# Full 128-row operands in the attention scores and the mLSTM selector, and the PV products of two heads issued together, in a two-layer decoder trunk

## The chip, the core and the metric

The kernel runs on one NeuronCore of a Trainium2 chip. The metric is the device time of one execution in microseconds (us). The kernel before took 924.36 us, the median of three runs (923.03 to 927.12). All durations below come from the profile of one execution of it.

The engines have short names: PE multiplies matrices (PEld is its loading of weights, which overlaps with the multiplying), DVE, ACT and POOL work elementwise, and SP starts the transfers of weights.

## What is computed

Two layers work on 256 tokens of width 1024. Each layer is a mixer (a matrix memory of 4 heads, called mLSTM, beside a sliding-window attention of 16 heads with 4 key heads) and an MLP. The part that matters here:

```python
def mixer_block(h, ...):
    proj = h @ w_in                       # D_MODEL x 6664
    ...
    hm = mlstm_chunkwise(mq, mk, mvf, ig, logf)
    ...
    ha = sliding_window_attention(aq..., ak..., av..., sinks, rel_bias)
    y = sigmoid(ga) * (hm @ w_branch_m) + sigmoid(gb) * (ha @ w_branch_a)
    return y @ w_out

def sliding_window_attention(q, k, v, sinks, rel_bias):   # 16 heads of 64, window 128
    scores = einsum(q, k) * A_HEAD_DIM ** -0.5
    logits = where(valid, scores + bias, -inf)
    m = maximum(max(logits), sink)
    p = exp(logits - m)
    denom = sum(p) + exp(sink - m)
    out = einsum(p / denom, v)
```

## The kernel before

**Products.** Every float32 operand of the large products is held as two float32r parts, high and low, and each product is three matmuls: high by high, low by high, high by low (L211 to L213 with 512 columns moving per matmul, L225 to L227 with 256; together they are called the stream below). ACT makes the high part of a piece of weights (L142), DVE the low part (L117; POOL does one piece of a layer), four pieces ahead of PE.

**Slots.** The program is a list of slots. A slot holds 24 stream matmuls of 256 columns or 12 of 512. Other work is tied to slots by number and is written ahead of the slot's products, so every engine's order is fixed by hand. `s_qk` is the first slot of the memory's queries and keys, and "slot n" below means `s_qk + n`.

**Attention.** Head h goes through four steps, with `heads_at` giving its slot:

- `att1` at slot `heads_at[h]`: four matmuls for the scores (L811 to L814), then bias, sink and maximum on DVE (L819, L821), and the exponentials on ACT (L824 to L826).
- `att2` one slot later: the division, on DVE and POOL (L832 to L835).
- `att3` three slots later: three transposes on PE (L841) and a copy of the result to a tile PT, on ACT (L846), or on DVE for heads 0 and 14 (L844). There are three PT tiles.
- `att4` four slots later: PT times the values, two float32 matmuls for each head (L858, L859), each of which the chip runs as two passes. The result of an even head lies in columns 0 to 63 of the array, that of an odd head in columns 64 to 127. Four heads fill one accumulator, which is then copied and split.

Scores, transposes and PV accumulators share four PSUM tiles, the "B" tiles.

**Operands of the scores.** In the tile q, the 64 rows of a head hold the high part of its queries, and the other 64 rows hold their low part. The tile `kh` holds the same high keys in both halves, so one matmul of 128 rows (L811, L813) gives high by high plus low by high. The low keys `kl` also stand in both halves, but L812 and L814 read only the head's own 64 rows.

**The memory's selector.** `mem1` of each of the 4 memory heads, at slots `s_ga + 2h + 1`, starts with a matmul of `sel` and `Rs` over 64 rows (L877). Rows 0 to 3 and 32 to 35 carry values; the others are zero. The four gates that feed `Rs` are computed on DVE around slots 4 to 6 (`gates2`, L690 to L705) and transposed on PE in slot 6 (`gates3`, L712, L713).

Of the kernel before, what the change touches and what calls it, by code (L numbers as in the profile page):

```python
# [12 lines left out]
F32R = mybir.dt.float32r  # L13
# [4 lines left out]
P = 128  # L18
T = 256
# [23 lines left out]
def trunk(ctx: ExitStack, tc: tile.TileContext, x, norm_mix_g, w_in, conv_w, conv_b, b_igate, b_fgate,  # L43
          mlstm_norm_g, attn_sinks, rel_bias, w_branch_m, w_branch_a, w_out, norm_mlp_g, w_up, w_down,
          final_norm_g, out):
    nc = tc.nc
    const = ctx.enter_context(tc.tile_pool(name="const", bufs=1))
# [19 lines left out]
    def tmp():  # L67
        return act.tile([P, 512], F32, tag="tmp", bufs=4, name=nm("tmp"))
# [12 lines left out]

# [1 line left out]
    N_RAW, N_SPL, AHEAD = 4, 7, 4  # L83
    pieces, pc, last_use, raws = [], {}, {}, {}
# [69 lines left out]

# [1 line left out]
    slots = []  # L156
# [3 lines left out]
    def slot(units, post=()):  # L160
        """units: list of (pieces needed, emit)."""
        slots.append((units, list(post)))
        i = len(slots) - 1
        for need, _ in units:
            for p_ in need:
                last_use[p_] = i
        return i
# [32 lines left out]

# [1 line left out]
    def xs(st, key, xT, pid, kt, tt, hf, first, last, w0=0, n=512):  # L202
        """st[key][:, :n] (+)= x[tt] @ n columns of a piece."""

        def emit():
            xh, xl = st[xT]
            wh, wl = pc[pid]
            b = st[key][:, :n]
            s = slice(tt * P, (tt + 1) * P)
            c = slice(w0 + hf * 512, w0 + hf * 512 + n)  # L210
            nc.tensor.matmul(b, xh[:, kt, s], wh[:, c], start=first, stop=False)  # L211
            nc.tensor.matmul(b, xh[:, kt, s], wl[:, c], start=False, stop=False)  # L212
            nc.tensor.matmul(b, xl[:, kt, s], wh[:, c], start=False, stop=last)  # L213

        return ([pid], emit)

    def ws(st, key, half, xT, pid, kt, wc, first, last):
        """half of st[key] (+)= (x @ 128 columns of a piece)^T, both token tiles."""

        def emit():  # L220
            xh, xl = st[xT]
            wh, wl = pc[pid]
            o = st[key][:, half * T : (half + 1) * T]
            c = slice(wc, wc + P)
            nc.tensor.matmul(o, wh[:, c], xh[:, kt, :], start=first and half == 0, stop=False, skip_group_check=True)  # L225
            nc.tensor.matmul(o, wh[:, c], xl[:, kt, :], start=False, stop=False, skip_group_check=True)  # L226
            nc.tensor.matmul(o, wl[:, c], xh[:, kt, :], start=False, stop=last, skip_group_check=True)  # L227

        return ([pid], emit)
# [4 lines left out]
    def xs_group(st, bkey, xT, w, c0, head="k", tail="k", k0=0, first=True, last=True, alloc=True):  # L234
        """8 slots; returns the first slot's index. head/tail: the order within kts 0-3 / 4-7."""
        pid = [piece(w, k0 + k, c0) for k in range(8)]
        start = len(slots)
# [28 lines left out]
    def ws_group(st, bkey, xT, w, c0, tail="b", head="k"):  # L266
        """8 slots; head/tail: the order within kts 0-3 / 4-7, by kt or by bank."""
        start = len(slots)
# [31 lines left out]

# [1 line left out]
    def evac_split(pt, hi, lo, scale=None):  # L302
# [17 lines left out]
    class Norm:  # L320
        """x * rsqrt(mean(x^2) + eps) * g for one token tile, in steps."""

# [26 lines left out]

# [1 line left out]
    X = const.tile([P, 2, D], F32, name="X")  # L351
# [15 lines left out]
    mask = const.tile([P, P], BF16, name="mask")  # L367
    sel = const.tile([64, 4], F32R, name="sel")
    Rs = const.tile([64, 384], F32R, name="Rs")
    cw = const.tile([P, 80], F32, name="cw")  # L370
# [33 lines left out]
    def setup_small():  # L404
# [4 lines left out]
        z = tmp()  # L409
        nc.gpsimd.memset(z, 0.0)  # L410
        nc.scalar.copy(Rs, z[:64, 0:384])
        for r in (0, 32):
            nc.gpsimd.affine_select(out=z[r : r + 32, 0:4], in_=z[r : r + 32, 0:4], pattern=[[-1, 4]],
                                    compare_op=ALU.not_equal, fill=1.0, base=0, channel_multiplier=1)
        nc.scalar.copy(sel, z[:64, 0:4])
        S0["b8"] = big8()
# [41 lines left out]

# [1 line left out]
    def boundary(st_prev, bkey, prev, st, xkey, nxt, gkey, xtag):  # L460
        """prev: first of the 4 closing slots (tile 0 half 0, 0/1, 1/0, 1/1); nxt: first slot that reads xT."""

# [51 lines left out]
    def first_norm(st, xtag, nxt):  # L514
        """The first norm's gain is applied per channel, after the transposes."""
        xh, xl = st["hT"] = xT_tiles(xtag)
# [63 lines left out]

# [1 line left out]
    def mixer(l, ta, tb):  # L582
        w = w_in[l]
        st = {}
# [11 lines left out]

        # attention keys and values, and both gates
        s_kv = len(slots)
        for k2 in range(4):
            pid = kv_piece(w, k2)  # L600
            units = []
            for kk in range(2):
                kt, w0 = 2 * k2 + kk, kk * 520
                f, e = kt == 0, kt == 7
# [27 lines left out]

        # attention queries
        s_aq = ws_group(st, "aq", "hT", w, AQ0)
# [19 lines left out]

        # gates of the matrix memory: log forget gates, running sums and maxima
        def s24():
# [66 lines left out]

        # memory queries and keys: causal convolution along time, then silu times two
        s_qk = ws_group(st, "qk", "hT", w, 0, tail="k", head="p")
# [33 lines left out]

        # output gate of the matrix memory  # L760
        s_mo = xs_group(st, "mo", "hT", w, MO0, tail="th")
# [42 lines left out]

        # sliding-window attention: a head goes through its four steps in five slots
        def att1(h):
            g, hs = h // 4, slice((h % 2) * 64, (h % 2) * 64 + 64)
            q, kh, kl = st[("q", h // 8)][:, h % 2 * 4 + h % 8 // 2, :], st["kh"], st["kl"]
            gk = g % 2 * 2 + g // 2
            sp = psB()  # L810
            nc.tensor.matmul(sp[:, 0:P], q[:, 0:P], kh[:, gk, 0:P], start=True, stop=False, skip_group_check=True)  # L811
            nc.tensor.matmul(sp[:, 0:P], q[hs, 0:P], kl[hs, gk, 0:P], start=False, stop=True, skip_group_check=True)  # L812
            nc.tensor.matmul(sp[:, P : 3 * P], q[:, P:T], kh[:, gk, :], start=False, stop=False, skip_group_check=True)  # L813
            nc.tensor.matmul(sp[:, P : 3 * P], q[hs, P:T], kl[hs, gk, :], start=False, stop=True,  # L814
                             skip_group_check=True)
            L = act.tile([P, 384], F32, tag="L", bufs=5, name=nm("L"))
# [31 lines left out]

        def att4(h):
            g, hh, hs = h // 4, h % 4, slice((h % 2) * 64, (h % 2) * 64 + 64)  # L850
            if h == 0:
                st["haT"] = xT_tiles(tb)
            if hh == 0:
                st["pv"] = psB()
            pv, PT, va, haT = st["pv"], st[("att", h)], st["va"], st["haT"]
            o = pv[hs, (hh // 2) * T : (hh // 2 + 1) * T]
            vs = slice(g * 64, (g + 1) * 64)
            nc.tensor.matmul(o, va[:, 0, vs], PT[:, 0:T], start=(hh < 2), stop=False, skip_group_check=True)  # L858
            nc.tensor.matmul(o[:, P:T], va[:, 1, vs], PT[:, T:384], start=False, stop=True, skip_group_check=True)  # L859
            if hh == 3:  # L860
                evac_split(pv.rearrange("p (m t) -> p m t", m=2), haT[0][:, 2 * g : 2 * g + 2, :],
                           haT[1][:, 2 * g : 2 * g + 2, :])

        heads_at = (2, 3, 4, 6, 7, 8, 8, 10, 11, 15, 15, 16, 16, 18, 19, 22)
        for h in range(16):
            at_late(s_qk + heads_at[h], lambda h=h: att1(h))
        steps = [(heads_at[h] + j, 4 - j, f, h) for h in range(16) for j, f in ((1, att2), (3, att3), (4, att4))]
        for i, _, f, h in sorted(steps, key=lambda t: (t[0], t[1], t[3])):
            at(s_qk + i, lambda f=f, h=h: f(h))

        # matrix memory, all chunks at once
        sc = 0.25 * 128.0 ** -0.5

        def mem1(h):
            cols, qk = st["cols"], st["qkT"]
            pw = psB()
            nc.tensor.matmul(pw[:, :384], sel[:, h : h + 1].to_broadcast([64, P]), Rs, start=True, stop=False,  # L877
                             skip_group_check=True)
# [5 lines left out]
            sp = psB()  # L884
            nc.tensor.matmul(sp[:, 0:T], qk[:, 4 + h, 0:P], qk[:, h, :], start=True, stop=True,
                             skip_group_check=True)
            nc.tensor.matmul(sp[:, T:384], qk[:, 4 + h, P:T], qk[:, h, P:T], start=False, stop=True,
                             skip_group_check=True)
# [66 lines left out]

# [1 line left out]
    def mlp(l, ta, tb):  # L957
# [68 lines left out]
    prev = None  # L1026
    firsts = []
    for l in range(DEPTH):
# [8 lines left out]
        prev = (stp, s_t)  # L1037
# [5 lines left out]

    # final norm
    stp, s_t = prev
# [50 lines left out]
```

## Time and profile before

| | |
|---|---|
| median of three runs | 924.36 us |
| lowest and highest run | 923.03, 927.12 us |
| span of the profiled execution | 924.4 us (its time is given only as this span) |
| mean granted TensorE clock | 0.994 |
| costliest group on DVE: low parts, L117 | 329.5 us in 274 |
| costliest group on ACT: high parts, L142 | 286.3 us in 280 |

How to read it: a matmul's duration in the trace includes the way through the array, and matmuls overlap. What a matmul costs is the distance from its start to the start of the next. In a row of the timeline the columns are the start, the duration, the engine, the line, the operation, the tiles written and read, the rows and columns of the operands, and the count; the bracket is idle time ahead of the instruction and what ended it.

### The profile page before, as it was taken

Reading aid. Unit: us, or ns where it says so; the run is one execution under the profiler, and the core shown is the slowest. Engines: PE = TensorE matmul, PEld = TensorE weight load, DVE = VectorE, ACT = ScalarE, POOL = GpSimd, SP = SyncE. Lnnn points to the kernel's source line nnn. Section 1 sums busy time; section 2 is a strip of 40 time slices with the busy share of each in tenths; the row PEclk is TensorE's granted clock in tenths of the full one; section 3 lists DMA queues with packets and bytes.
Section 4 is the critical chain, followed back from the end, with each engine's and each line's share of the span. In section 5 each row is a group of like instructions: output and inputs, shape, how many; then the busy total and the mean of one; then the engine's idle time right before and its main releaser. Section 6 shows DMA issues by size and latency. Waiting matters only on the chain.

```text
span 924.4 us, 14901 instructions
## 1 busy us (share of the span) xinstructions
PE 907.8 (98%) x5837; PEld 804.3 (87%) x5837; DVE 574.9 (62%) x922; ACT 469.0 (51%) x769; POOL 137.0 (15%) x179
## 2 busy tenths in 40 slices
PE   8899999999999999999999999999999999999996
PEld 6789878999988999999889987789999889999985
DVE  6647677766677646464665676686666666546462
ACT  6465466655444635354445546666543454545351
POOL 3272343211000000000000533231200000000000
PEclk9999999999999999999999999999999999999999
DMA  7975252444555666464746444243455576565631
GB/s 233 248 231 182 92 154 75 138 138 145 199 176 157 212 206 212 154 227 138 236 134 205 157 149 126 92 144 113 165 154 179 182 228 218 166 212 169 214 115 46
DMA packets 46406, 155.27 MB, mean 168 GB/s; under 512 B 7192, under 2 KB 7296, under 8 KB 46336
## 3 DMA queue, kind: packets, MB, share of 16 engines
q1 hardware_dynamic: 44256, 148.46, 50.2%
q0 software_dynamic: 1792, 5.34, 2.2%
q8 instruction: 46, 0.75, 0.3%
q10 hardware_dynamic: 288, 0.52, 0.1%
q14 instruction: 24, 0.20, 0.1%
HBM read 153.23 MB, written 1.07 MB: 167 GB/s over the span
## 4 chain that ended last, share of the span: by engine, by line
PE 90%; DMA 3%; DVE 3%; issue 2%; POOL 1%; ACT 1%; POOLq 0%; SPq 0%; ACTq 0%; DVEq 0%
PE pa L211 12%; PE pa L212 12%; PE pa L213 12%; PE pa L225 10%; PE pa L226 9%; PE pa L227 9%; PE pb L226 5%; PE pb L225 5%; PE pb L227 5%; PE pb L858 2%; DMA raw<-in_w_in 1%; PE pb L841 1%; DMA b<-ed 1%; PE pb L813 1%; PE pb L313 1%
## 5 line engine op out<-in xcount | busy, mean ns | idle before, releaser
L117 DVE TENSOR_TENSOR lo<-raw,hi 128x1024 fp32r<-128x1024 f32 (+1 forms) x274 | 329.5, 1224 | 144.8 <-ACT hi L142 143.9
L142 ACT CAST hi<-raw 128x1024 fp32r<-128x1024 f32 (+1 forms) x280 | 286.3, 1049 | 179.4 <-PE pa L213 46.2
L225 PE MATMUL pa<-xh,hi 128*128 128x256 f32 x800 | 231.7, 290 | 4.1 <-ACT vm L593 2.8
L227 PE MATMUL pa<-xh,lo 128*128 128x256 f32 x800 | 225.4, 282 | 0.8 <-DVE lo L117 0.8
L226 PE MATMUL pa<-xl,hi 128*128 128x256 f32 x800 | 226.0, 283 | 0.0
L211 PE MATMUL pa<-hi,xh 128*128 128x512 f32 (+1 forms) x416 | 163.5, 393 | 0.1
L212 PE MATMUL pa<-lo,xh 128*128 128x512 f32 (+1 forms) x416 | 160.8, 387 | 0.7 <-DVE lo L117 0.7
L213 PE MATMUL pa<-hi,xl 128*128 128x512 f32 (+1 forms) x416 | 160.4, 386 | 0.0
L225 PEld LDWEIGHTS pa<-xh,hi 128*128 128x128 f32 x800 | 152.1, 190 | 8.1 <-ACT vm L593 3.2
L227 PEld LDWEIGHTS pa<-xh,lo 128*128 128x128 f32 x800 | 152.0, 190 | 1.0 <-DVE lo L117 1.0
L226 PEld LDWEIGHTS pa<-xl,hi 128*128 128x128 f32 x800 | 152.3, 190 | 0.3
L225 PE MATMUL pb<-xh,hi 128*128 128x256 f32 x384 | 108.2, 282 | 0.0
L226 PE MATMUL pb<-xl,hi 128*128 128x256 f32 x384 | 107.5, 280 | 0.0
L227 PE MATMUL pb<-xh,lo 128*128 128x256 f32 x384 | 107.4, 280 | 0.0
L213 PEld LDWEIGHTS pa<-hi,xl 128*128 128x128 f32 x416 | 78.3, 188 | 16.8
L212 PEld LDWEIGHTS pa<-lo,xh 128*128 128x128 f32 x416 | 78.4, 189 | 16.3 <-DVE lo L117 1.9
L211 PEld LDWEIGHTS pa<-hi,xh 128*128 128x128 f32 x416 | 78.3, 188 | 16.1 <-issue 0.3
L340 POOL TENSOR_TENSOR sm<-sm,mhalf 128x1 f32<-128x1 f32 x10 | 7.4, 744 | 505.2 <-DVE sm L339 505.2
L226 PEld LDWEIGHTS pb<-xl,hi 128*128 128x128 f32 x384 | 72.4, 188 | 1.7
L225 PEld LDWEIGHTS pb<-xh,hi 128*128 128x128 f32 x384 | 72.2, 188 | 1.8
L227 PEld LDWEIGHTS pb<-xh,lo 128*128 128x128 f32 x384 | 72.2, 188 | 0.0
L211 PE MATMUL pa<-hi,b 128*128 128x512 f32 x128 | 50.4, 394 | 0.0
(204 smaller groups left out, 1019.5 us busy)
## 6 DMA issues: line engine op xcount, KB each, us to landing
raw<-in_w_in SPq DMA_DIRECT2D x104, 512.0 KB, 4.1
raw<-in_w_up SPq DMA_DIRECT2D x64, 512.0 KB, 4.9
raw<-in_w_down SPq DMA_DIRECT2D x64, 512.0 KB, 4.3
raw<-in_w_branch_a SPq DMA_DIRECT2D x16, 512.0 KB, 3.6
raw<-in_w_branch_m SPq DMA_DIRECT2D x16, 512.0 KB, 3.7
raw<-in_w_out SPq DMA_DIRECT2D x16, 512.0 KB, 4.6
b<-ed POOLq DMA_DIRECT2D x2, 1024.0 KB, 9.3
g<-in_mlstm_norm_g POOLq DMA_DIRECT2D x2, 512.0 KB, 6.5
```

The costliest lines, as they stand in the source:

```text
L117: (eng or nc.vector).tensor_tensor(lo[:, :n], raw[:, :n], hi[:, :n].bitcast(F32), op=ALU.subtract)
L142: nc.scalar.copy(hi[:, :n], raw[:, :n])
L211: nc.tensor.matmul(b, xh[:, kt, s], wh[:, c], start=first, stop=False)
L212: nc.tensor.matmul(b, xh[:, kt, s], wl[:, c], start=False, stop=False)
L213: nc.tensor.matmul(b, xl[:, kt, s], wh[:, c], start=False, stop=last)
L225: nc.tensor.matmul(o, wh[:, c], xh[:, kt, :], start=first and half == 0, stop=False, skip_group_check=True)
L226: nc.tensor.matmul(o, wh[:, c], xl[:, kt, :], start=False, stop=False, skip_group_check=True)
L227: nc.tensor.matmul(o, wl[:, c], xh[:, kt, :], start=False, stop=last, skip_group_check=True)
L313: nc.tensor.transpose(pt[:, j * P : (j + 1) * P], src[:, j * P : (j + 1) * P], ident)
L813: nc.tensor.matmul(sp[:, P : 3 * P], q[:, P:T], kh[:, gk, :], start=False, stop=False, skip_group_check=True)
L841: nc.tensor.transpose(tp[:, j * P : (j + 1) * P], L[:, j * P : (j + 1) * P], ident)
L858: nc.tensor.matmul(o, va[:, 0, vs], PT[:, 0:T], start=(hh < 2), stop=False, skip_group_check=True)
```

## The change

Three edits. First, L812 and L814 read all 128 rows of q and `kl` instead of 64, which adds the term low by low to the scores. Second, `sel` and `Rs` have 128 rows, the added ones zero, and L877 becomes a matmul over 128 rows. Third, `att4` takes two heads: it is called for the even heads only, at the slot in which the odd head's `att4` stood, and writes the PV matmuls of both heads one after the other.

```diff
-    sel = const.tile([64, 4], F32R, name="sel")
-    Rs = const.tile([64, 384], F32R, name="Rs")
+    sel = const.tile([P, 4], F32R, name="sel")
+    Rs = const.tile([P, 384], F32R, name="Rs")
...
-        nc.scalar.copy(Rs, z[:64, 0:384])
+        nc.scalar.copy(Rs, z[:, 0:384])
...
-        nc.scalar.copy(sel, z[:64, 0:4])
+        nc.scalar.copy(sel, z[:, 0:4])
...
         def att1(h):
...
-            nc.tensor.matmul(sp[:, 0:P], q[hs, 0:P], kl[hs, gk, 0:P], start=False, stop=True, skip_group_check=True)
+            nc.tensor.matmul(sp[:, 0:P], q[:, 0:P], kl[:, gk, 0:P], start=False, stop=True, skip_group_check=True)
...
-            nc.tensor.matmul(sp[:, P : 3 * P], q[hs, P:T], kl[hs, gk, :], start=False, stop=True,
-                             skip_group_check=True)
+            nc.tensor.matmul(sp[:, P : 3 * P], q[:, P:T], kl[:, gk, :], start=False, stop=True, skip_group_check=True)
...
-        def att4(h):
+        def att4(h0):
...
-            o = pv[hs, (hh // 2) * T : (hh // 2 + 1) * T]
-            nc.tensor.matmul(o, va[:, 0, vs], PT[:, 0:T], start=(hh < 2), stop=False, skip_group_check=True)
-            nc.tensor.matmul(o[:, P:T], va[:, 1, vs], PT[:, T:384], start=False, stop=True, skip_group_check=True)
-            if hh == 3:
+            c = slice((h0 % 4 // 2) * T, (h0 % 4 // 2 + 1) * T)
+            for h in (h0, h0 + 1):
+                hs = slice((h % 2) * 64, (h % 2) * 64 + 64)
+                o, PT = pv[hs, c], st[("att", h)]
+                nc.tensor.matmul(o, va[:, 0, vs], PT[:, 0:T], start=(h0 % 4 == 0), stop=False, skip_group_check=True)
+                nc.tensor.matmul(o[:, P:T], va[:, 1, vs], PT[:, T:384], start=False, stop=True, skip_group_check=True)
+            if h0 % 4 == 2:
...
-        steps = [(heads_at[h] + j, 4 - j, f, h) for h in range(16) for j, f in ((1, att2), (3, att3), (4, att4))]
+        steps = [(heads_at[h] + j, 4 - j, f, h) for h in range(16) for j, f in ((1, att2), (3, att3))]
+        steps += [(heads_at[h + 1] + 4, 0, att4, h) for h in range(0, 16, 2)]
...
-            nc.tensor.matmul(pw[:, :384], sel[:, h : h + 1].to_broadcast([64, P]), Rs, start=True, stop=False,
+            nc.tensor.matmul(pw[:, :384], sel[:, h : h + 1].to_broadcast([P, P]), Rs, start=True, stop=False,
```

The rows below are the program's own order on PE; a bracket names the engine whose semaphore the instruction waits for. In the changed kernel L841 has become L840, L858 and L859 have become L860 and L861. On the other engines the order of the instructions is as it was.

In slot 6 of the first layer, behind the transposes of the gates (L712, L713), there stood before: the PV matmuls of head 0 (L858, L859), the transposes of head 1 (L841) and the scores of head 3 (L811).

```order
L713 MATMUL pb_1206<-ident,b_180_1108 128x4
L858 MATMUL pb_1217<-PT_1169,va_606 64x256 [waits DVE_49]
L859 MATMUL pb_1217<-PT_1169,va_606 64x128
L841 MATMUL pb_1220<-ident,L_1061 128x128 [waits Pool_49] x2
L841 MATMUL pb_1220<-ident,L_1061 128x128
L811 MATMUL pb_1229<-kh_648,b_144_840 128x128 [waits PE_49]
```

With the change the PV matmuls are gone from this place, and the B tiles fall otherwise: the scores of head 3 take the tile that DVE last read for the scores of head 2.

```order
L713 MATMUL pb_1206<-ident,b_180_1108 128x4
L840 MATMUL pb_1215<-ident,L_1061 128x128 [waits PE_49,Pool_49]
L840 MATMUL pb_1215<-ident,L_1061 128x128 [waits Pool_49]
L840 MATMUL pb_1215<-ident,L_1061 128x128
L811 MATMUL pb_1224<-kh_648,b_144_840 128x128 [waits DVE_49]
```

The wait for PT of head 0 has moved away from this slot, and a wait for DVE stands at L811 instead.

In slot 7, one slot on, the piece of the difference behind the slot's stream is this (PT_1169 is head 0's in both, PT_1224 and PT_1219 are head 1's):

```order
-L858 MATMUL pb_1217<-PT_1224,va_606 64x256
-L859 MATMUL pb_1217<-PT_1224,va_606 64x128
-L841 MATMUL pb_1273<-ident,L_1128 128x128 x3
+L860 MATMUL pb_1268<-PT_1169,va_606 64x256
+L861 MATMUL pb_1268<-PT_1169,va_606 64x128
+L860 MATMUL pb_1268<-PT_1219,va_606 64x256
+L861 MATMUL pb_1268<-PT_1219,va_606 64x128
+L840 MATMUL pb_1273<-ident,L_1128 128x128 x3
```

Here one head's PV matmuls have become two heads', ahead of the transposes of head 2.

In slot 12 PV matmuls of two heads stood next to each other before too, of heads 5 (PT_1483) and 6 (PT_1489); now they are those of heads 4 and 5:

```order
-L858 MATMUL pb_1476<-PT_1483,va_606 64x256
-L859 MATMUL pb_1476<-PT_1483,va_606 64x128
-L858 MATMUL pb_1476<-PT_1489,va_606 64x256
-L859 MATMUL pb_1476<-PT_1489,va_606 64x128
+L860 MATMUL pb_1529<-PT_1440,va_606 64x256
+L861 MATMUL pb_1529<-PT_1440,va_606 64x128
+L860 MATMUL pb_1529<-PT_1480,va_606 64x256
+L861 MATMUL pb_1529<-PT_1480,va_606 64x128
```

The place and the number of matmuls are the same; the heads differ. Over a layer, PV matmuls stood at 13 places before (at three of them two heads'), and stand at 8 now.

More of the change, by code (lines that the diff above doesn't have):

```diff
@@ L806, in att1 @@
         def att1(h):
-            g, hs = h // 4, slice((h % 2) * 64, (h % 2) * 64 + 64)
+            g = h // 4
             q, kh, kl = st[("q", h // 8)][:, h % 2 * 4 + h % 8 // 2, :], st["kh"], st["kl"]
@@ L847, in att3 @@
             st[("att", h)] = PT
-        def att4(h):
-            g, hh, hs = h // 4, h % 4, slice((h % 2) * 64, (h % 2) * 64 + 64)
-            if h == 0:
+        def att4(h0):
+            g = h0 // 4
+            if h0 == 0:
                 st["haT"] = xT_tiles(tb)
-            if hh == 0:
+            if h0 % 4 == 0:
                 st["pv"] = psB()
-            pv, PT, va, haT = st["pv"], st[("att", h)], st["va"], st["haT"]
-            o = pv[hs, (hh // 2) * T : (hh // 2 + 1) * T]
+            pv, va, haT = st["pv"], st["va"], st["haT"]
             vs = slice(g * 64, (g + 1) * 64)
-            nc.tensor.matmul(o, va[:, 0, vs], PT[:, 0:T], start=(hh < 2), stop=False, skip_group_check=True)
-            nc.tensor.matmul(o[:, P:T], va[:, 1, vs], PT[:, T:384], start=False, stop=True, skip_group_check=True)
-            if hh == 3:
+            c = slice((h0 % 4 // 2) * T, (h0 % 4 // 2 + 1) * T)
[5 more added lines that the diff above has]
+            if h0 % 4 == 2:
                 evac_split(pv.rearrange("p (m t) -> p m t", m=2), haT[0][:, 2 * g : 2 * g + 2, :],
```

## The prediction

> **What bounds the kernel now.** First the page's shares of the engines, then the chain of work that ended last.
>
> ```profile
> span 924.4 us, 14901 instructions
> PE 907.8 (98%) x5837; PEld 804.3 (87%) x5837; DVE 574.9 (62%) x922; ACT 469.0 (51%) x769; POOL 137.0 (15%) x179
> PE 90%; DMA 3%; DVE 3%; issue 2%; POOL 1%; ACT 1%; POOLq 0%; SPq 0%; ACTq 0%; DVEq 0%
> ```
>
> PE is busy in 98% of the span and is 90% of the chain. Time that PE saves in the middle is therefore time of the kernel, as long as the others can follow. The sum is made against this span, 924.4 us, which equals the median of the three runs. Next I read PE's timeline at the places that the change touches, by distances from start to start. Head 0's scores in the first layer:
>
> ```profile
> 82.45 0.28 PE L227 MATMUL pa<-xh,lo 128*128 128x256 f32 x1
> 82.57 0.22 PE L811 MATMUL pb<-kh,b 128*128 128x128 f32 x1
> 82.72 0.32 PE L812 MATMUL pb<-kl,b 64*128 64x128 f32 x1
> 82.97 0.38 PE L813 MATMUL pb<-kh,b 128*128 128x256 f32 x1
> 83.28 0.38 PE L814 MATMUL pb<-kl,b 64*128 64x256 f32 x1
> 83.60 0.39 PE L225 MATMUL pa<-xh,hi 128*128 128x256 f32 x1
> 83.82 0.28 PE L226 MATMUL pa<-xl,hi 128*128 128x256 f32 x1
> ```
>
> In the stream, matmuls of 256 columns start 0.12 us apart (82.45 to 82.57). Around the half-row matmuls the distances are 0.15, 0.25, 0.31, 0.32 and, into the stream, 0.22. Each change between 64 and 128 rows costs up to 0.2 us beyond the matmul's own time, in either direction: L813 and L225, with 128 rows themselves, are late as well.
>
> **The change part by part.**
>
> *Scores.* From L811's start to L226's start there are 1.25 us for five matmuls. With one row count I take each at the stream's 0.117 (0.12 in the rows, which have two places), also the 128-column ones, because a weight load sets them:
>
> ```profile
> L811 PEld LDWEIGHTS pb<-kh,b 128*128 128x128 f32 x32 | 6.0, 189 | 1.6 <-DVE b L737 0.3 <-issue 0.3
> L858 PEld LDWEIGHTS pb<-PT,va 128*64 128x64 f32 x64 | 5.1, 134 | 7.2 <-issue 2.5 <-DVE PT L844 1.7 <-ACT b L752 0.7
> ```
>
> A load of 128 columns takes 55 ns more than one of 64, so 128 columns take about 110 ns. That gives 5 x 0.117 = 0.585, and a saving of 1.25 - 0.585 = 0.667 us a head; x32 heads (the count of L811) = **21.3 us**. Bounds: nothing, if the distance isn't due to the rows; and, if a 128-column matmul can follow in half of a 256-column one's time, 64 x 0.06 = 3.8 us more. I take the loads' value, the nearest row. The Trainium skill's page "TensorE: Matmul & The Clock Gate", section "Back-to-back issue gap", gives about 81 ns for loads and matmuls of 128 columns in a stream; by it the sum would be an estimated 2.3 us larger, and no row here shows such a stream.
>
> *PV.* A place with one head's PV matmuls, and the place in slot 12 with two heads':
>
> ```profile
> 178.38 0.28 PE L227 MATMUL pa<-xh,lo 128*128 128x256 f32 x1
> 178.59 0.65 PE L858 MATMUL pb<-PT,va 128*64 128x256 f32 x2
> ...
> 179.38 0.39 PE L225 MATMUL pa<-xh,hi 128*128 128x256 f32 x1
> 179.60 0.28 PE L226 MATMUL pa<-xl,hi 128*128 128x256 f32 x1
> ```
>
> ```profile
> 130.62 0.40 PE L212 MATMUL pa<-lo,xh 128*128 128x512 f32 x1
> 130.85 0.40 PE L213 MATMUL pa<-hi,xl 128*128 128x512 f32 x1
> 131.18 0.66 PE L858 MATMUL pb<-PT,va 128*64 128x256 f32 x4
> 131.66 0.40 PE L859 MATMUL pb<-PT,va 128*64 128x128 f32 x4
> 131.98 0.50 PE L211 MATMUL pa<-hi,xh 128*128 128x512 f32 x1
> ```
>
> One head: 178.38 to 179.60 is 1.22, less two stream distances (0.235) = 0.985 us. Without the step back into the stream, 178.38 to 179.38 less one distance, it is 0.88. Two heads: 130.85 to 131.98 is 1.13, less one distance of 0.23 (512 columns, 130.62 to 130.85) = 0.90 us. The second head is all but free. All four L858 passes start before the first L859, though the program writes head 5's L858 and L859 ahead of head 6's: the two halves of the array's columns run side by side. The change leaves 8 places with two heads where there were 10 with one and 3 with two. A layer saves 5 x 0.985 - 5 x 0.025 = 4.8 us; two layers **9.6 us**.
>
> *Selector.*
>
> ```profile
> 202.76 0.27 PE L227 MATMUL pa<-xh,lo 128*128 128x256 f32 x1
> 202.97 0.44 PE L877 MATMUL pb<-Rs,sel 64*128 64x384 f32 x1
> 203.34 0.23 PE L879 MATMUL pb<-mask,identb 128*128 128x128 bf16 x1
> L877 PE MATMUL pb<-Rs,sel 64*128 64x384 f32 x8 | 3.5, 437 | 0.0
> ```
>
> From L227 to L879 0.58 us; with full rows 0.117 + 0.117 x 384/256 = 0.29. The saving is 0.285, x8 = **2.3 us**. The two wider copies of zeros to Rs and sel I cost at nothing: ACT is idle half the time. Uncovered they could add at most their own time again, and an ACT instruction takes 0.6 us in the mean (469.0 us by 769 on the page). Gross saving: 21.3 + 9.6 + 2.3 = **33.2 us**.
>
> *The waits that come.* The program order gives two. At slot 6 the scores of head 3 now wait until DVE has read those of head 2, and at slot 7 the pair waits for PT of head 1. In the second layer, PE first and then the others:
>
> ```profile
> 548.57 0.20 PE L713 MATMUL pb<-ident,b 4*128 4x4 f32 x1
> 549.45 0.65 PE L858 MATMUL pb<-PT,va 128*64 128x256 f32 x2 [0.68 <-DVE PT L844]
> ...
> 554.69 0.65 PE L858 MATMUL pb<-PT,va 128*64 128x256 f32 x2
> ```
>
> ```profile
> 542.45 2.52 POOL L117 TENSOR_TENSOR lo<-raw,hi 128x1024 fp32r<-128x1024 f32 x1
> 542.77 2.47 DVE L696 TENSOR_TENSOR b<-b 4x256 f32<-4x256 f32 x1
> ...
> 548.65 0.08 DVE L821 DVE_READ_ACCUMULATOR2_ANT sm<- 128x1 f32 x1
> 552.53 0.48 ACT L846 COPY PT<-pb 128x384 f32<-128x384 f32 x1
> ```
>
> DVE's work on the gates stands still beside POOL's L117 (2.47 beside 2.52 us), and POOL comes to that piece by ACT's and DVE's queues, not by PE's pace. So DVE's read, which ends at 548.73, stays where it is. PE, earlier by three heads' scores (2.0 us), would be through with the gates' and head 1's transposes near 547.0 (548.57 - 2.0, and 0.4 for them) and waits 1.8 us, where it waited 0.7 before. Behind the waiting L811 all of PE's stream is queued, and DVE and ACT wait for that. The copy of PT for head 1 (to 553.01) hangs on the same DVE chain: the pair's second head can start at about 553.07, against 554.69 before. PE's own savings to that point would be 4 x 0.667 + 0.985 = 3.65; it gets 1.62. **Lost: 2.0 us.** In the first layer (the last row is a stretch of time: its length, the busy time and count of PE, PEld, DVE, ACT and POOL, the granted clock, the DMA share and GB/s):
>
> ```profile
> 102.48 0.47 ACT L846 COPY PT<-pb 128x384 f32<-128x384 f32 x1
> 106.17 0.65 PE L858 MATMUL pb<-PT,va 128*64 128x256 f32 x2
> 101.60:105.00 3.40, 3.40 (x17) 3.38 (x17) 2.68 (x8) 2.55 (x8) 1.48 (x1) 0.50 0.43 143
> ```
>
> 102.95 against 106.17 allows 3.2 of the 3.65: **0.4 lost**. The granted clock was 0.50 for 3.4 us there; 24 stream matmuls took from 101.60 to 106.17 instead of 24 x 0.117 = 2.8. Of the 1.75 between, 0.2 go to the steps out of L814 and into L858, and 1.5 to the clock. It lies behind the wait of slot 6; after a longer wait it may come in either layer, in both, or in none. I keep one, and 1.5 us either way for the range.
>
> *Can the others follow?*
>
> ```profile
> 82.00:192.00 110.00, 109.19 (x686) 91.13 (x685) 75.95 (x190) 62.16 (x149) 33.69 (x33) 0.98 0.42 129
> 140.00:165.00 25.00, 25.00 (x156) 20.58 (x155) 19.14 (x60) 15.65 (x41) 9.15 (x10) 1.00 0.28 85
> ```
>
> DVE is busy 76 of 110 us in the first layer's attention, which becomes 110 - 33.2/2 = 93 us, so 81%. In the densest 25 us it is 19.1; PE would take about 4.3 less (five heads' scores, one PV place), and DVE is then busy 19.1 of 20.7. It fits with little left, and what PE needs most often, the pieces of weights, is made four ahead. I take nothing, and up to 4 us a layer for the range. Net: 33.2 - 2.4 = 30.8, so 924.4 - 30.8 = **893.6 us**.
>
> **The rivals.**
>
> *A: the heads of a pair run one after the other.* The skill's page named above, section "Part 3: Packing small matmuls", says that matmuls start and end strictly in program order. As a mechanism here: head two's passes start behind head one's last. For it: nothing in the rows; slot 12 speaks against it, with four L858 ahead of L859. Price: a lone place runs 0.79 us from L858 to L225, of which leaving the column half takes about 0.09, so 0.7 for each of 16 pairs, 11 us: 905 us.
>
> *B: DVE and ACT don't follow.* For it speaks the 19.1 of 25 us; against it the four pieces ahead. Price 2 to 4 us a layer: 898 to 902 us.
>
> *C: 128-column matmuls follow faster.* 893.6 - 3.8 = 890 us.
>
> *D: it doesn't do what it says: the distances around L812, L814 and L877 belong to something else, such as accumulating into the same PSUM tile.* Against it: the stream accumulates three times into one tile at 0.12. Then 21.3 and 2.3 fall away: 915 us; with A too, no change.
>
> *E: slower.* The pairs wait for PT of the odd head at every place as at slot 7, since the copy on ACT now ends PE's slot. This decides from 33.2/16 = 2.1 us a pair; with a whole slot's wait (24 x 0.117 = 2.8) it is 924.4 + 16 x 2.8 - 33.2 = 936 us. Against it: in slot 7 the copy ends 1.7 us ahead of L858 (553.01, 554.69), and elsewhere PE's own transposes lead to the copy, so it moves along with PE.
>
> **How the numbers follow.** Forecast 0.61 (891 to 898 us), A 0.05, B 0.18, C 0.07, D 0.04 with a time still below 919.8, no change 0.03, E 0.02. A measurement of this kernel can tell about 0.5%, 4.6 us, from no change. Faster is 0.61 + 0.05 + 0.18 + 0.07 + 0.04 = 0.95, same 0.03, slower 0.02. The range from 889.5 to 903 us holds the forecast, B and C, with the clock's 1.5 us, and leaves out A, D, E and no change, together 0.14.
>
> **What would show it.** Right: L812 and L814 with 128 rows and all five distances near 0.12; eight places in a layer with L860 x4; L877 to its next about 0.18; idle time of PE ahead of L811 in slot 6, ended by DVE, and ahead of the pair in slot 7. Wrong: distances above 0.2 at full rows (D); a pair near 1.7 us (A); idle time of PE behind DVE's L117 or ACT's copies in slots 14 to 20 (B). A shorter distance than 0.117 between L811 and L812 makes it C.

## The result, and the profile after

The changed kernel took 893.92 us, the median of four runs (891.90 to 896.61); the kernel before took 923.94 us beside it (four runs, 923.03 to 927.12). The ratio is 0.967, with a 95% interval from 0.964 to 0.970. The profiled execution took 891.90 us; its span is 890.0 us. The forecast was 893.6 us.

The page after, the engines and the chain of work that ended last:

```profile
span 890.0 us, 14901 instructions
PE 874.9 (98%) x5837; PEld 790.4 (89%) x5837; DVE 574.2 (65%) x922; ACT 466.6 (52%) x769; POOL 138.9 (16%) x179
PE 88%; DMA 4%; DVE 3%; issue 2%; ACT 1%; POOL 1%; POOLq 0%; SPq 0%; ACTq 0%; DVEq 0%
```

As many instructions as before, and DVE, ACT and POOL are as busy as before. PE's busy time fell by 32.9 us, and the span with it, by 34.4.

PE's timeline after, at four places: head 0's scores, one of the places with a pair, the pair of slot 7, and the selector.

```profile
81.14 0.22 PE L811 MATMUL pb<-kh,b 128*128 128x128 f32 x1
81.19 0.28 PE L812 MATMUL pb<-kl,b 128*128 128x128 f32 x1
81.31 0.33 PE L813 MATMUL pb<-kh,b 128*128 128x256 f32 x1
81.48 0.28 PE L814 MATMUL pb<-kl,b 128*128 128x256 f32 x1
81.59 0.28 PE L225 MATMUL pa<-xh,hi 128*128 128x256 f32 x1
81.71 0.28 PE L226 MATMUL pa<-xl,hi 128*128 128x256 f32 x1
...
99.62 0.65 PE L860 MATMUL pb<-PT,va 128*64 128x256 f32 x2
100.10 0.38 PE L861 MATMUL pb<-PT,va 128*64 128x128 f32 x2
100.41 0.65 PE L860 MATMUL pb<-PT,va 128*64 128x256 f32 x2
100.89 0.38 PE L861 MATMUL pb<-PT,va 128*64 128x128 f32 x2
...
119.93 0.40 PE L213 MATMUL pa<-hi,xl 128*128 128x512 f32 x1
120.25 0.66 PE L860 MATMUL pb<-PT,va 128*64 128x256 f32 x4
120.73 0.40 PE L861 MATMUL pb<-PT,va 128*64 128x128 f32 x4
121.06 0.50 PE L211 MATMUL pa<-hi,xh 128*128 128x512 f32 x1
...
184.65 0.27 PE L227 MATMUL pa<-xh,lo 128*128 128x256 f32 x1
184.76 0.34 PE L880 MATMUL pb<-Rs,sel 128*128 128x384 f32 x1
184.94 0.23 PE L882 MATMUL pb<-mask,identb 128*128 128x128 bf16 x1
```

From L811 to the second matmul of the stream there are 0.57 us instead of 1.25. The pair runs its four L860 passes ahead of the first L861, except in slot 7, where the two heads run one after the other. From the stream to L882 there are 0.29 us instead of 0.58.

What PE waits for inside the attention is one line after, the scores of head 3 in slot 6, once in each layer (total, count, longest). The first row below is of after, the second of before.

```profile
PE pb L811 <- DVE sm L820: 1.1, 2, 0.6
```

```profile
PE pb L858 <- DVE PT L844: 1.5, 2, 0.8
```

The span can be cut at head 0's scores in each layer, since PE's program is the same up to there. The starts of the second layer's (the first layer's are shown) are, after and before:

```profile
514.04 0.22 PE L811 MATMUL pb<-kh,b 128*128 128x128 f32 x1
```

```profile
532.74 0.22 PE L811 MATMUL pb<-kh,b 128*128 128x128 f32 x1
```

| stretch, us | before | after | shorter by |
|---|---|---|---|
| start to head 0's scores | 82.57 | 81.14 | 1.43 |
| from there to the same place in the second layer | 450.17 | 432.90 | 17.27 |
| from there to the end | 391.66 | 375.96 | 15.70 |

The first row isn't the change's. In three profiled executions of the changed kernel head 0's scores start at 81.14, 81.19 and 80.56, and in two of another kernel of this study at 82.35 and 84.92, so one kernel's start varies by 2.5 us or more. What varies there wasn't looked into. The second row holds about 1.5 us of the half-speed clock that the profiled execution of before has in its first layer; after has no such stretch in the attention. What is left, about 15.7 us in each layer, is the change's: 31.4 us.

### The profile page after: what moved, and what is told of

Its sections match the earlier page's. It is cut to its first block, busy times and chain, and to the rows that moved or that the text cites. A ratio compares the mean times of both kernels' runs of the same rounds, so it can differ in the third digit from the quotient of the medians.

```text
span 890.0 us, 14901 instructions
## 1 busy us (share of the span) xinstructions
PE 874.9 (98%) x5837; PEld 790.4 (89%) x5837; DVE 574.2 (65%) x922; ACT 466.6 (52%) x769; POOL 138.9 (16%) x179
## 4 chain that ended last, share of the span: by engine, by line
PE 88%; DMA 4%; DVE 3%; issue 2%; ACT 1%; POOL 1%; POOLq 0%; SPq 0%; ACTq 0%; DVEq 0%
PE pa L211 13%; PE pa L213 13%; PE pa L212 13%; PE pa L226 9%; PE pa L225 9%; PE pa L227 9%; PE pb L226 5%; PE pb L225 5%; PE pb L227 5%; DMA raw<-in_w_in 2%; PE pb L840 1%; PE pb L860 1%; DMA b<-ed 1%; PE pb L313 1%; PE pb L900 1%
## 5 line engine op out<-in xcount | busy, mean ns | idle before, releaser
L117 DVE TENSOR_TENSOR lo<-raw,hi 128x1024 fp32r<-128x1024 f32 (+1 forms) x274 | 329.5, 1224 | 139.5 <-ACT hi L142 137.5
L225 PE MATMUL pa<-xh,hi 128*128 128x256 f32 x800 | 228.6, 286 | 3.0 <-ACT vm L593 3.0
L226 PE MATMUL pa<-xl,hi 128*128 128x256 f32 x800 | 225.0, 281 | 0.0
L211 PE MATMUL pa<-hi,xh 128*128 128x512 f32 (+1 forms) x416 | 163.3, 392 | 1.5 <-ACT xh L531 1.5
L213 PE MATMUL pa<-hi,xl 128*128 128x512 f32 (+1 forms) x416 | 161.4, 388 | 0.0
L225 PEld LDWEIGHTS pa<-xh,hi 128*128 128x128 f32 x800 | 150.9, 189 | 4.1 <-ACT vm L593 3.5
L226 PEld LDWEIGHTS pa<-xl,hi 128*128 128x128 f32 x800 | 151.2, 189 | 0.3
L225 PE MATMUL pb<-xh,hi 128*128 128x256 f32 x384 | 108.2, 282 | 0.0
L226 PE MATMUL pb<-xl,hi 128*128 128x256 f32 x384 | 107.5, 280 | 0.0
L211 PEld LDWEIGHTS pa<-hi,xh 128*128 128x128 f32 x416 | 78.9, 190 | 17.0 <-ACT xh L531 1.6
L213 PEld LDWEIGHTS pa<-hi,xl 128*128 128x128 f32 x416 | 78.8, 189 | 16.8
L226 PEld LDWEIGHTS pb<-xl,hi 128*128 128x128 f32 x384 | 72.4, 188 | 1.7
L225 PEld LDWEIGHTS pb<-xh,hi 128*128 128x128 f32 x384 | 72.2, 188 | 1.8
L211 PE MATMUL pa<-hi,b 128*128 128x512 f32 x128 | 50.4, 394 | 0.0
```

The lines of the kernel that those rows point to most:

```text
L117: (eng or nc.vector).tensor_tensor(lo[:, :n], raw[:, :n], hi[:, :n].bitcast(F32), op=ALU.subtract)
```

## The experiments

Each ran on one chip beside the kernel before, whose median there is given. In these kernels the line numbers behind L814 differ by up to three from those of the changed one.

### The three edits apart

The scores alone: L812 and L814 read all rows, as in the change; nothing else is changed.

> The kernel before with the scores alone changed (L812 and L814 over 128 rows, low by low added). Theory, that each change of row count costs PE time: from L811's start to the stream's first matmul 0.46 us instead of 1.03, and 0.10 less behind it, so 32 x 0.67 = 21.5 us, less up to 1 us a layer because PT of head 0 comes no earlier: 903 us, 901 to 905. Rival, that the distances belong to accumulating into one PSUM tile: they stay above 0.2 and the time stays at 924 us.

908.9 us (906.89 to 909.65) against 926.01: 0.9815, interval 0.9785 to 0.9844. The distances are those of after (0.457 us from L811 to L225), so the gain at the scores is there; yet the kernel is 17.1 us faster, not 21.7, and the time lies outside the 901 to 905 us expected. Two rows of its waits, and two windows of its profile in the second layer, show where the rest went (in the windows the granted clock is the third number from the right):

```profile
PE pb L858 <- DVE PT L844: 3.6, 2, 1.9
PE pb L713 <- DVE b L703: 0.9, 1, 0.9
```

```profile
534.50:537.89 3.39, 1.12 (x10) 0.81 (x8) 3.03 (x14) 0.51 (x2) 0.00 (x0) 1.00 0.50 155
537.89:544.72 6.83, 6.35 (x27) 5.63 (x28) 4.49 (x13) 4.71 (x14) 2.54 (x3) 0.50 0.28 79
```

PE waits for PT of head 0 in slot 6 for 2.1 us more than before, and 0.9 us for the gates (L713), where it had no wait before; and the clock is then halved for 6.83 us. In those windows PE has little to do and then runs at half speed: a saving ahead of a wait is given back at it. The 21.7, less 3.0 for the waits and 3.2 for the clock (half of PE's 6.35 busy us), and with the 1.5 that the profile of before lost to its own half-speed stretch, make 17.0; from head 0's scores to the end of PE's work the two profiles differ by 17.7. That the wait is the reason is a guess until it is taken away, so the next kernel does that.

The scores alone, and the PV product of head 0 one slot later:

```diff
-        steps = [(heads_at[h] + j, 4 - j, f, h) ...
+        steps = [(heads_at[h] + j + (j == 4 and h == 0), 4 - j, f, h) ...
```

> The kernel with the scores alone on full rows, and one edit more: the PV product of head 0 alone moves from slot 6 to slot 7, so that PE no longer waits in slot 6 for PT of head 0. Theory (the scores alone gained 17 us on their own chip instead of 21 to 23 because that wait grew to 1.8 us a layer, and the clock was halved behind it): the wait goes, a shorter one of 0.3 to 1.1 us for DVE's read of head 2's scores comes in its place, and the two heads together in slot 7 save 0.3 us a layer besides; 3 us less without the clock event and up to 6 less with it: 902 to 906 us, ratio to before 0.976 to 0.980. Rival (the scores save less than their distances show, and the wait isn't the reason): 908 to 909, ratio 0.981 to 0.983.

902.44 us (901.34 to 905.10) against 924.53: 0.9752, interval 0.9731 to 0.9773. It lies below the interval of the scores alone, by 0.6% or about 5.8 us, within the theory's 3 to 6. In its profile the wait for PT is gone, and PE waits 2.5 us in slot 6 of the two layers together, for the gates and for DVE's read, where with the scores alone it waited 4.4. A stretch of 3.41 us at half clock is left there in the second layer, in an execution that was the slowest of the five. So moving head 0's PV away brought the lost gain back; how much of that was the wait, how much the clock behind it, and how much the two heads standing together in slot 7 (0.6 us by the theory) can't be told from single profiles. The kernel also shows that the edits aren't independent: pairing takes head 0's PV out of slot 6, and with it the wait that faster scores run into.

The pairs alone:

> The kernel before with the PV matmuls of two heads issued together, and nothing else. Theory, that the two halves of the columns run side by side: five PV places fewer in a layer at 0.97 us each, 9.6 us in all, less 0.7 us a layer if the pair in slot 7 still runs one after the other behind the copy of PT of head 1: 915 us, 913 to 918. Rival, that matmuls start in program order: a pair costs 0.7 us more than one head, and the time is 924 us or above.

914.44 us (912.75 to 916.45) against 926.01: 0.9881, interval 0.9854 to 0.9908. 11.6 us were gained; the PV places explain 9.6, the wait for PT in slot 6, which is gone from the list of waits, 1.5. With slower scores the pair of slot 7 isn't late:

```profile
101.54 0.69 PE L861 MATMUL pb<-PT,va 128*64 128x256 f32 x4
```

The selector alone:

> The kernel before with the selector alone over 128 rows (zeros added). Theory: 0.285 us for each of 8, 2.3 us: 921.7 us, at the edge of what three rounds can tell; in the trace L877 to L879 falls from 0.37 to 0.18 us and the matmul ahead of it loses 0.09. Rival, that the 384 columns set it: nothing moves in the trace.

922.48 us (920.31 to 925.10) against 926.01: 0.9965, interval 0.9946 to 0.9983. That is 1.6 to 5.0 us by the interval, and the forecast was 2.3. Its places, measured start to start as at the scores, went from 1.29 to 1.01 us, 8 x 0.28 = 2.2.

### Is it the row count, and not the half-row matmul itself?

Before, with the two full-row matmuls first: the same four matmuls, but two changes of the row count in a head instead of four.

```diff
-            nc.tensor.matmul(sp[:, 0:P], q[hs, 0:P], kl[hs, gk, 0:P], start=False, stop=True, ...)
             nc.tensor.matmul(sp[:, P : 3 * P], q[:, P:T], kh[:, gk, :], start=False, stop=False, ...)
+            nc.tensor.matmul(sp[:, 0:P], q[hs, 0:P], kl[hs, gk, 0:P], start=False, stop=True, ...)
```

> Before, with one edit: the two full-row score matmuls of a head (L811, L813) come first and the two half-row ones (L812, L814) behind them, so that the row count changes twice a head instead of four times; the number and size of the matmuls stay. Theory (what costs is the change of the row count, a quarter of 0.677 us each): 2 x 0.169 x 32 heads = 10.8 us less at PE, of which about 1 us a layer is lost again to the wait for PT of head 0 in slot 6, so 914 to 916 us. Rival 1 (a half-row matmul is slow in itself, however they are ordered): the same as before, 924. Rival 2 (writing the same PSUM region twice in a row is what is slow): saves as much as the theory or more in the distances at L812 and L814, but none at the step back into the stream. The distances from the stream's last matmul to the second one after the scores add up to 1.25 before; theory 0.9, rival 1 1.25.

916.82 us (914.84 to 921.15) against 924.35: 0.9917, interval 0.9888 to 0.9945. Head 0's scores, in the order in which they now run (L812 has full rows, L813 half):

```profile
82.52 0.22 PE L811 MATMUL pb<-kh,b 128*128 128x128 f32 x1
82.57 0.33 PE L812 MATMUL pb<-kh,b 128*128 128x256 f32 x1
82.84 0.33 PE L813 MATMUL pb<-kl,b 64*128 64x128 f32 x1
83.00 0.33 PE L814 MATMUL pb<-kl,b 64*128 64x256 f32 x1
83.26 0.39 PE L225 MATMUL pa<-xh,hi 128*128 128x256 f32 x1
83.48 0.28 PE L226 MATMUL pa<-xl,hi 128*128 128x256 f32 x1
```

From L811 to L226 there are now 0.96 us, between before's 1.25 and after's 0.57, though as many half-row matmuls run. So the order decides, and the rival that a half-row matmul is slow in itself falls as the main cause: between the two half-row ones, where the row count stays, there are 0.16 us, and 0.12 between the same sizes with full rows after (81.19 to 81.31). The second rival, that writing one region twice is slow, falls with after: there L811 and L812 write one region 0.05 us apart. The changes don't cost the same, though: the two that are gone were worth 0.29 us, the two that are left 0.39. My theory took a quarter of the sum for each, and its range ended 0.8 us below the median. By the trace, 32 x 0.285 = 9.1 us less the wait for PT, which grew from 1.5 to 2.9, is 7.7; 7.5 were measured.

### Do two column halves run side by side, or do fewer places make the gain?

The changed kernel with heads h and h + 2 as a pair: as many places, but both heads in the same column half.

```diff
-            for h in (h0, h0 + 1):
+            for h in (h0, h0 + 2):
...
-        steps += [(heads_at[h + 1] + 4, 0, att4, h) for h in range(0, 16, 2)]
+        steps += [(heads_at[h + 2] + 4, 0, att4, h) for h in range(16) if h % 4 < 2]
```

> The changed kernel with heads h and h + 2 in a pair instead of h and h + 1: the same PV matmuls at 8 places of a layer, but both heads of a pair in the same half of the columns. Theory, that two heads are nearly free only because they use different halves: every pair runs one after the other, 1.7 us a place instead of 1.0 at the seven places of a layer that overlap now, 14 x 0.7 = 9.8 us more than the changed kernel: 904 us, 902 to 906. Rival, that only the number of places counts: 894 us.

902.83 us (902.16 to 904.31) against 926.01: 0.9757, interval 0.9733 to 0.9780. One of its places:

```profile
123.25 0.40 PE L213 MATMUL pa<-hi,xl 128*128 128x512 f32 x1
123.58 0.65 PE L860 MATMUL pb<-PT,va 128*64 128x256 f32 x2
124.06 0.38 PE L861 MATMUL pb<-PT,va 128*64 128x128 f32 x2
124.28 0.59 PE L860 MATMUL pb<-PT,va 128*64 128x256 f32 x2
124.71 0.38 PE L861 MATMUL pb<-PT,va 128*64 128x128 f32 x2
125.02 0.50 PE L211 MATMUL pa<-hi,xh 128*128 128x512 f32 x1
```

From L213 to L211 1.77 us, against 1.13 after: 0.64 for each of the 14 pairs that run side by side after is 9.0 us. The first pair of a layer ran one head after the other after too, and takes 0.14 us less here than there; but it stands in slot 8 now, and in slot 7 PE waits for POOL, which it does not after:

```profile
PE pb L841 <- POOL L L835: 1.5, 2, 0.7
```

9.0 + 1.5 - 0.3 = 10.2 us; from head 0's scores to the end of PE's work the two kernels differ by 10.15. Eight places with both heads in one half take as long together as the 13 places of before (8 x 1.64 = 13.1 us, against 10 x 0.985 + 3 x 1.0 = 12.9). The gain of pairing is therefore the running side by side, not the smaller number of places.

### The pair of slot 7, and versions beyond the change

The changed kernel, first as the reference for the two versions after it, and again as that for the last two:

> The changed kernel once more, as the reference for the two versions beside it: 893.9 us (891.5 to 896.5), 0.967 of before. The trace should again show two PE waits for DVE at the scores of head 3 in slot 6 (0.3 to 0.8 us each), and the slot-7 pair in two parts.

> The changed kernel again, on the same chip as the two versions with four heads: 893 us (892 to 895.5), so 1 to 2 us above them.

892.92 us (892.21 to 895.40) against 924.35, and 893.08 us (892.44 to 894.77) against 925.96: 0.9658 and 0.9646. The profile of the second has a wait of 1.0 us for DVE (L703) at the gates' transposes of slot 6 that the first's hasn't.

The first pair one slot later:

```diff
-        steps += [(heads_at[h + 1] + 4, 0, att4, h) for h in range(0, 16, 2)]
+        steps += [(heads_at[h + 1] + (5 if h == 0 else 4), 0, att4, h) for h in range(0, 16, 2)]
```

> The changed kernel with the first pair of each layer (heads 0 and 1) one slot later, in slot 8 instead of 7. Theory (the pair of slot 7 runs in two parts only because PT of head 1 is ready too late): the pair now shows four L860 passes ahead of the first L861, its place costs 1.0 instead of 1.7 us, and the kernel is 1.4 us faster than the changed one: 892.5, ratio to it 0.9984. Rival (the pair's second head is late for another reason, or the saved time comes back as a longer wait in a later slot): two parts again, or no gain.

893.62 us (893.19 to 895.39): no gain beside 892.92. The pair does run side by side now, as the theory says, but a wait stands in slot 7 that the trace of the changed kernel doesn't have:

```profile
101.47 0.44 PE L841 MATMUL pb<-ident,L 128*128 128x128 f32 x2 [0.74 <-POOL L L835]
...
105.08 0.66 PE L861 MATMUL pb<-PT,va 128*64 128x256 f32 x4
```

The pair in slot 7 was cover: while it ran, POOL finished the division of head 2's scores. The rival was right.

All four heads of a group at one place, with the transposed result put back into the head's own score tile for want of room:

```diff
+            PT = L
...
+            for h in range(h0, h0 + 4):
...
+        steps += [(heads_at[h + 3] + 4, 0, att4, h) for h in range(0, 16, 4)]
```

> The changed kernel with the PV products of all four heads of a group in one place, at the slot of the last of them; the result of the transposes goes back to the head's score tile (8 of them instead of 5), since PT tiles for five heads don't fit. Theory (a place has a fixed cost, the steps into and out of the 64-column form, near 0.3 us; the passes themselves cost 0.35 us a head when two column halves run side by side): a place of four heads costs 1.7 us, against 2 x 1.0 for two places; 8 places fewer save 2.4 us, and the slot-7 pair's 1.4 us go too, so 890 us (888.5 to 892), ratio to the changed kernel 0.996. Rival 1 (no fixed cost: a place of four takes 2.0): 892.5. Rival 2 (the longer place holds up the transposes and scores behind it, and DVE and ACT fall behind): 894 to 897 with new waits of PE behind the pairs.

> The version with four heads at one place again, as the reference: 891.5 us (891 to 893), two waits of PE for POOL of 0.7 us in slot 7.

891.52 us (891.25 to 892.62) beside 892.92, and on the second chip 893.49 us (890.40 to 894.80) beside 893.08, outside the 891 to 893 expected and not 1 to 2 us below the changed kernel. A gain isn't shown. The place itself does cost what was expected, 1.70 us (start to start) instead of twice 1.00, and from head 0's scores to the end of PE's work both profiled executions have 801.0 us, against 801.9 to 803.5 in three of the changed kernel. Of the expected 3.8 us about 1 is left: the same wait for POOL takes 0.7 us a layer back, and one for ACT in slot 9 another 0.3.

The same, with the transposes of head 2 moved from slot 7 to slot 8, away from POOL:

> The version with four heads' PV products at one place, and one edit more: the transposes of head 2 move from slot 7 to slot 8, so that PE no longer waits in slot 7 for POOL's division of head 2's scores (0.74 us a layer there). Theory (that wait is what took back the gain of the slot-7 pair): the wait of PE for POOL in slot 7 is gone, 1.5 us less than the version with four heads: 890.0 us (888.5 to 891). Rival (the next thing is late by as much, such as ACT's copies in slots 8 and 9, on which PE waits 0.3 us already): no gain, with the wait of PE at the start of slot 9 for ACT (L739) grown from 0.3 to 0.8 us or more.

893.09 us (891.91 to 894.70) beside 893.49 and 893.08: no gain. The wait for POOL is gone, and this stands in its place at the start of slot 9:

```profile
107.27 0.50 PE L211 MATMUL pa<-hi,xh 128*128 128x512 f32 x1 [1.24 <-ACT b L739]
```

It had been 0.3 us before the move. In slots 6 to 9 DVE, POOL and ACT are now each in turn the next to be late, and none of the three ways tried of moving PE's work about there gained anything. No version beats the changed kernel by more than can be measured.

## Why the prediction was right

**The scores: right, and by the mechanism named.** 1.134 us (own matmuls and the step back into the stream) became 0.457: 0.677 a head, forecast 0.667. The row-count changes were the cause: the reordered halves show it, and rival D falls. The distances aren't five times 0.117, as I had put it: after the 128-column L811 the next matmul follows in 0.05 us, and then L813 to L814 takes 0.17. So the weight load of 128 columns, which I had at about 110 ns, did not set the distance behind L811. Rival C was right at one place and was paid back at the next; its 3.8 us became 0.3. The Trainium skill's page "TensorE: Matmul & The Clock Gate", section "Wait — 56ns, not 53.3ns?", gives 55.6 ns from start to start for 128 columns; the 0.05 agrees with it.

**PV: right.** A pair's place takes 1.003 us; the forecast was 0.985 + 0.025. Seven of eight places in a layer run side by side. Rival A, one head after the other, is the kernel with both heads in one column half; it costs 0.64 us a pair, where the rival had 0.7. The same page's section "Part 3: Packing small matmuls" has matmuls start and end strictly in program order; here the second head's L860 starts ahead of the first head's L861, and the measurement decides.

**Selector: right.** 1.293 to 1.008 us a place, 0.285 as forecast. The gross sum is thus 21.7 + 9.6 + 2.3 = 33.6, forecast 33.2.

**The waits: the places were right, the sizes were not.** The step "DVE's read, which ends at 548.73, stays where it is" failed. These are ACT, POOL, DVE and PE after, in the second layer:

```profile
516.05 1.05 ACT L142 CAST hi<-raw 128x1024 fp32r<-128x1024 f32 x1 [2.33 <-DMA raw<-in_w_in]
...
522.88 0.41 DVE L696 TENSOR_TENSOR b<-b 4x256 f32<-4x256 f32 x1
523.00 2.59 POOL L117 TENSOR_TENSOR lo<-raw,hi 128x1024 fp32r<-128x1024 f32 x1
523.33 2.54 DVE L697 TENSOR_TENSOR_SCAN b<-b 4x128 f32<-4x128 f32 x1
...
528.83 0.08 DVE L820 DVE_READ_ACCUMULATOR2_ANT sm<- 128x1 f32 x1
...
528.97 0.33 PE L811 MATMUL pb<-kh,b 128*128 128x128 f32 x1 [0.50 <-DVE sm L820]
```

```profile
535.69 1.05 ACT L142 CAST hi<-raw 128x1024 fp32r<-128x1024 f32 x1 [3.27 <-DMA raw<-in_w_in]
```

Counted from head 0's scores, DVE's read ended at 15.99 us before (548.73 - 532.74) and at 14.87 after (528.91 - 514.04), 1.1 earlier. POOL's piece came 0.75 earlier too (9.71 and 8.96), and ACT's piece of weights, which waits for its transfer and whose row of before is the second one, 0.94 earlier (2.95 and 2.01). So PE waited 0.50 us at L811 and not 1.8. Other profiles show that the transfer and PE's earlier gates were both needed for that. In the last profile of the changed kernel (the second of the two references above) head 0's scores of the second layer start at 513.46 and PE reaches the gates as early as after, but the piece of weights came at 3.57:

```profile
517.03 1.05 ACT L142 CAST hi<-raw 128x1024 fp32r<-128x1024 f32 x1 [3.89 <-DMA raw<-in_w_in]
528.26 0.22 PE L713 MATMUL pb<-ident,b 4*128 4x4 f32 x1 [1.04 <-DVE b L703]
529.83 0.33 PE L811 MATMUL pb<-kh,b 128*128 128x128 f32 x1 [0.74 <-DVE sm L821]
```

There DVE's read ended at 16.32, and PE waited 1.78 us in all, as the prediction had it. With the pairs alone, in the first layer, the piece came early (2.05), but PE reached the gates 1.37 us later than after, and the read ended at 16.12. So whether this wait is short depends also on when a transfer lands, which differs by 1.5 us between the three profiles of the changed kernel (2.01, 2.07 and 3.57); what moves it wasn't looked into.

The other wait came as described. In slot 7 the second head of the pair starts when PT of head 1 is there, which in the first layer is

```profile
99.88 0.47 ACT L845 COPY PT<-pb 128x384 f32<-128x384 f32 x1
```

to 100.35, and the head follows at 100.41. Up to that start, PE should have gained 4 x 0.677 + 0.985 = 3.69. In the second layer it gained 2.75 (554.69 - 532.74 before, 533.24 - 514.04 after), so 0.94 was lost where I had 2.0. In the first layer it gained 4.33, or about 2.8 without the clock's 1.5, so 0.9 was lost where I had 0.4. The sum is 1.8 against 2.4: two errors of opposite sign.

**The clock.** I kept one stretch at half speed; the profiled execution after has none in the attention. That is the 1.5 us that the range allowed.

**The others follow.** No wait of PE for DVE, ACT or POOL lies in slots 14 to 20. In the densest stretch DVE is busy 22.5 of 25 us:

```profile
140.00:165.00 25.00, 25.00 (x215) 23.69 (x214) 22.47 (x52) 16.99 (x38) 10.73 (x10) 1.00 0.54 166
```

That is 90%, where I had 19.1 of 20.7. Rival B didn't come there. Where it nearly came is slots 6 to 9, as the versions beyond the change show. Rival E came in slot 7 alone, at 0.8 us a layer.

**The sum and its base.** Net forecast 30.8; the trace gives 31.4 without the start and the clock, and the medians 30.0. I had taken the span of 924.4 for the same as the median of the runs. In the runs where both are known the time is about 2 us above the span (893.72 with 891.9; before, 924.35 with 922.3), so that execution took about 2 us longer than the median, and these 2 us stood in for the step from span to time. The forecast was close to the median for that reason too, and that part is luck.

## What to carry to other kernels

On TensorE, count the changes between operand shapes, not only the matmuls. In a stream of full-row matmuls, a small product over 64 rows cost about 0.3 us more here than the same product over full rows; where the other rows can be filled with zeros, or with a term that is harmless, full rows are worth trying. Products that use different column halves belong next to each other in the program, and their operands must be ready together. And when PE is made faster ahead of a fixed chain on other engines, look first at what PE waits for next: one edit alone can give back a fifth of its gain at a wait that another edit removes.

## What the runs showed of the hardware

- Two products in different column halves run side by side although the program has them in turn: four passes of L860 start ahead of L861, 1.00 us for a place instead of 1.64.
- A change of the row count between 64 and 128 costs 0.14 to 0.2 us, by the two that the reordering took out (0.29 together) and the two that it left (0.39), one of which is the step back into the stream.
- Inside the attention the clock was halved for 3.41 us or for 6.83, in the kernel with the scores alone behind a stretch in which PE was busy 1.12 of 3.39 us. That little work ahead leads to it isn't a rule. Three windows of before, each 3.41 us long (PE's busy time is the second number):

```profile
33.40:36.81 3.41, 1.63 (x8) 0.98 (x6) 2.14 (x2) 1.67 (x2) 0.00 (x0) 1.00 1.03 349
36.81:40.22 3.41, 2.37 (x17) 2.15 (x18) 3.14 (x5) 3.31 (x5) 0.00 (x0) 1.00 0.80 247
98.22:101.63 3.41, 2.60 (x17) 1.79 (x16) 1.99 (x9) 2.11 (x6) 0.97 (x2) 1.00 0.00 1
```

The first, with 1.63 us of work, was followed by full speed, the last, with 2.60, by the half speed of the prediction's window from 101.60. What decides stays open.
- A short DVE instruction can be held for nearly the whole of a POOL one, and which one is hit depends on a few tenths of a microsecond: before, L696 took 2.47 us beside POOL's L117; after, L696 was through in 0.41 and the next one, L697, took 2.54.
